# Seven products in place of plain tiles for one more pair in the last pass of a down projection

## The chip, the cores and the metric

The kernel runs on one core of a Trainium2 chip. The metric is the device time of one execution in microseconds (us). A TensorE matmul (PE) takes a stationary tile of 128x128 and a moving tile of 128x512; VectorE is called DVE, ScalarE ACT, GpSimd POOL, and SP is the engine that issues most of the loads.

## The reference

One layer on 256 rows of width 2048: a mixing block (differential attention and a convolution), and then a gated feed-forward block. Only the end of the second one is touched by the change:

```python
h = h + mixed @ w_out
hn = rms_norm(h, norm2_g)
a, bu = hn @ w_gate, hn @ w_up            # 2048 -> 5632
h = h + (silu(a) * bu) @ w_down           # 5632 -> 2048
```

Everything is float32.

## The kernel before

**Precision.** PE multiplies a rounded float32 type. So each operand is split into a rounded part (hi) and the rest (lo), and a product of two tiles is three matmuls: hi by hi, lo by hi, hi by lo. ACT makes the hi part of a weight tile with a cast; its lo part comes from DVE (the raw tile minus hi) or, where a letter in the order below is a capital, from ACT (the negative of hi's input) and a DMA of POOL that adds the raw weights once more (line 346).

**The feed-forward block.** The 5632 hidden columns are taken in 11 blocks of 512 (numbers 0 to 10), in three groups of 4, 4 and 3 blocks. After each group's gate and up blocks a pass of w_down multiplies what the group has made. In a pass the output's 2048 columns are taken in two halves of 1024, called here half A and half B. A hidden block gives two *pairs* of k-tiles, written (8, 0) and (8, 1) for block 8. The third pass has six: (8, 0), (8, 1), (9, 0), (9, 1), (10, 0), (10, 1).

**Two ways to multiply a pair.** In one half a pair is a 2x2 block product: two row blocks of 128, two k-tiles, two column blocks of 512.

- As a *plain pair* it is two units, "g" and "u" (the two column blocks), of four products each: 12 matmuls a unit, 24 in all. Letters G and U are the same with the lo part of the weights by DMA. One unit's weights are a 512 KB load (`raw`); ACT casts `whi` (L342), DVE makes `wlo` (L351).
- As a *seven-product pair*, unit "s" (a 2x2 scheme of Strassen's kind), it is 7 products, 21 matmuls on L1094 to L1096. Its weights are one 1 MB load (`wb`), and then DVE adds up four sums `wt` (L1061, L1062, L1063), ACT casts `wh` (L1068 and L1072), and DVE makes `wl` (L1076 and L1077). `wb`, `wh` and `wl` have two buffers each, `wt` one. The other operand needs sums as well: the function `pair_forms` copies the transposed activations to `af`, casts them, makes the sums `fs` (L975 to L978), lo parts (L979, L980), a cast of `fs` (ACT, L982) and the lo part of it (L984). A plain pair's activations take a copy and a cast (L955, L957) and one subtraction (L959).

**From a gate and up block to w_down.** When the last matmul of block 10 is done, DVE finishes its gated product (L1215 and L1217, two of each). PE transposes it (L922, four small matmuls for each pair), and `transposed` makes the operands, pair (10, 0) first, then (10, 1).

**What sets the order.** Each engine works through one queue in the order in which the program was written. That order is made by `run_chunks`: before it writes the matmuls of unit t it writes the preparation of units ahead of it (the lo parts of up to three units ahead, the sums `wt` of up to five). Work that comes from activations, such as `transposed`, is a generator; one step of it is written at fixed places inside the matmuls (four in an "s" unit, two in a plain one), and `lag(n)` lets n such places go by. A unit whose activations are not yet written makes the generators go on until they are:

```python
while not c["ready"](c):
    resume()
```

The order of the units is a string for each half. `so_far`, a read of the output so far, shares the buffer of `wt` and is used at the very end.

Of the kernel before, what the change touches and what calls it, by code (L numbers as in the profile page):

```python
# [89 lines left out]

DOWN = (dict(pairs=((1, 0), (1, 1), (2, 0)), order=("sgGsgGgsuUuUu",) * 2),
        dict(pairs=((4, 0), (4, 1), (5, 0)), order=("sgGsgGgsuUuUu",) * 2),
        dict(pairs=((8, 0), (8, 1), (9, 0)), order=("sGsGgsUUu", "sGsGGsUUu")))

RAW_AHEAD = 5
LOAD_AHEAD, DMA_AHEAD, SUMS_AHEAD, HI_AHEAD, LO_AHEAD = 9, 5, 5, 4, 3
# [1244 lines left out]
```

## Time and profile before

| | us |
|---|---|
| median of 3 runs | 1040.02 (1039.77 to 1040.20) |
| profiled execution, its own time | 1041.07 |
| its span on the core | 1039.2 |
| mean granted clock of TensorE | 0.998 |
| PE busy | 1030.1 (99%) |
| DVE busy | 862.3 (83%) |
| ACT busy | 685.6 (66%) |
| POOL busy | 155.4 (15%) |

Matmuls overlap in the profile: each is shown for some 390 ns, though the next one starts sooner. A busy PE of 99% says that it hardly ever waits; the time that one matmul costs is the distance between two starts.

### The profile page before, as it was taken

Reading aid. Unit: us, or ns where it says so; the run is one execution under the profiler, and the core shown is the slowest. Engines: PE = TensorE matmul, PEld = TensorE weight load, DVE = VectorE, ACT = ScalarE, POOL = GpSimd, SP = SyncE. Lnnn points to the kernel's source line nnn. Section 1 sums busy time; section 2 is a strip of 40 time slices with the busy share of each in tenths; the row PEclk is TensorE's granted clock in tenths of the full one; section 3 lists DMA queues with packets and bytes.
Section 4 is the critical chain, followed back from the end, with each engine's and each line's share of the span. In section 5 each row is a group of like instructions: output and inputs, shape, how many; then the busy total and the mean of one; then the engine's idle time right before and its main releaser. Section 6 shows DMA issues by size and latency. Waiting matters only on the chain.

```text
span 1039.2 us, 13042 instructions
## 1 busy us (share of the span) xinstructions
PE 1030.1 (99%) x4641; PEld 850.3 (82%) x4641; DVE 862.3 (83%) x1086; ACT 685.6 (66%) x864; POOL 155.4 (15%) x198
## 2 busy tenths in 40 slices
PE   8999999999999999999999999999999999999998
PEld 6888888888888888788888888888888888888886
DVE  5599989898546699999978789999896697998983
ACT  5855568766856567777556567776765666767761
POOL 0040133411100101001002120010001121101021
PEclk9999999999999999999999999999999999999999
DMA  9867766676566669898889998987969999879896
GB/s 357 302 202 211 238 206 213 187 211 176 163 201 231 230 215 281 241 323 240 257 246 298 257 306 267 309 229 249 307 187 285 300 271 331 235 243 298 250 249 129
DMA packets 65777, 258.05 MB, mean 248 GB/s; under 512 B 7344, under 2 KB 8624, under 8 KB 58288
## 3 DMA queue, kind: packets, MB, share of 16 engines
q1 hardware_dynamic: 48656, 201.34, 53.5%
q0 software_dynamic: 16768, 55.58, 28.2%
q8 instruction: 36, 0.59, 0.2%
q10 hardware_dynamic: 288, 0.29, 0.1%
q14 instruction: 29, 0.24, 0.1%
HBM read 248.80 MB, written 8.39 MB: 247 GB/s over the span
## 4 chain that ended last, share of the span: by engine, by line
PE 95%; DVE 2%; ACT 1%; issue 1%; DMA 1%; POOL 0%; SPq 0%; DVEq 0%
PE q L1116 11%; PE q L1120 11%; PE q L1115 11%; PE acc L387 11%; PE acc L382 11%; PE acc L381 11%; PE q L1094 9%; PE q L1096 8%; PE q L1095 8%; PE ps_a L922 1%; DMA raw<-in_wts_dram 1%; PE ps_s L731 1%; PE ps_o L809 0%; DVE y L596 0%; PE ps_h L859 0%
## 5 line engine op out<-in xcount | busy, mean ns | idle before, releaser
L342 ACT CAST whi<-raw 128x1024 fp32r<-128x1024 f32 (+1 forms) x261 | 270.3, 1046 | 105.1 <-PE acc L382 42.0
L351 DVE TENSOR_TENSOR wlo<-raw,whi 128x1024 fp32r<-128x1024 f32 (+1 forms) x173 | 209.0, 1218 | 72.9 <-ACT whi L342 71.4
L381 PE MATMUL acc<-whi,lhi 128*128 128x512 f32 x416 | 164.7, 396 | 1.5 <-ACT lhi L243 1.4
L382 PE MATMUL acc<-whi,llo 128*128 128x512 f32 x416 | 162.8, 391 | 0.7 <-DVE llo L244 0.7
L1077 DVE TENSOR_TENSOR wl<-wt,wh 128x2048 fp32r<-128x2048 f32 x58 | 132.7, 2287 | 20.6 <-ACT wh L1072 20.6
L1068 ACT CAST wh<-wb 128x1536 fp32r<-128x1536 f32 x58 | 86.0, 1483 | 87.5 <-PE q L1095 49.1
L346 POOL DMA_DIRECT2D wlo<-in_wts_dram x74 | 65.0, 889 | 510.4 <-ACT wlo L345 483.6
L1115 PE MATMUL q<-whi,chi 128*128 128x512 f32 x320 | 124.7, 390 | 0.0
L1116 PE MATMUL q<-whi,clo 128*128 128x512 f32 x320 | 124.6, 389 | 0.0
L1072 ACT CAST wh<-wt 128x2048 fp32r<-128x2048 f32 x58 | 110.4, 1904 | 18.5 <-DVE wt L1063 18.4
L1094 PE MATMUL q<-wh,fhi 128*128 128x512 f32 x280 | 109.2, 390 | 0.4 <-DVE sum L1199 0.4
L1096 PE MATMUL q<-wl,fhi 128*128 128x512 f32 x280 | 109.0, 389 | 0.0
L1095 PE MATMUL q<-wh,flo 128*128 128x512 f32 x280 | 109.0, 389 | 0.0
L596 DVE SCALAR_TENSOR_TENSOR y<-upad,cw,y 128x256 f32<-128x256 f32 x240 | 100.8, 488 | 5.3 <-ACT y L589 5.3
L1076 DVE TENSOR_TENSOR wl<-wb,wh 128x1536 fp32r<-128x1536 f32 x58 | 101.6, 1752 | 2.3 <-ACT wh L1068 2.3
L387 PE MATMUL acc<-wlo,lhi 128*128 128x512 f32 x368 | 101.4, 397 | 0.2 <-DVE wlo L351 0.2
L381 PEld LDWEIGHTS acc<-whi,lhi 128*128 128x128 f32 x416 | 78.5, 189 | 18.5 <-ACT lhi L243 1.8
L382 PEld LDWEIGHTS acc<-whi,llo 128*128 128x128 f32 x416 | 78.5, 189 | 17.3 <-DVE llo L244 1.2
L1120 PE MATMUL q<-wlo,chi 128*128 128x512 f32 x320 | 86.9, 393 | 0.0
L387 PEld LDWEIGHTS acc<-wlo,lhi 128*128 128x128 f32 x368 | 68.9, 189 | 14.6 <-DVE wlo L351 0.6
L345 ACT ACTIVATE wlo<-raw 128x1024 fp32r<-128x1024 f32 x74 | 78.1, 1056 | 0.0
L1061 DVE TENSOR_TENSOR wt<-wb 128x1024 f32<-128x1024 f32 x58 | 70.8, 1221 | 1.8 <-DMA wb<-in_wts_dram 1.3
(224 smaller groups left out, 1732.5 us busy)
## 6 DMA issues: line engine op xcount, KB each, us to landing
raw<-in_wts_dram SPq DMA_DIRECT2D x259, 512.0 KB, 5.6
wb<-in_wts_dram SPq DMA_DIRECT2D x57, 1024.0 KB, 8.1
wlo<-in_wts_dram POOLq DMA_DIRECT2D x74, 512.0 KB, 9.3
lod<-in_wts_dram POOLq DMA_DIRECT2D x14, 512.0 KB, 5.8
out_dram<-sum POOLq DMA_DIRECT2D x22, 256.0 KB, 7.2
h<-in_x_dram SPq DMA_DIRECT2D x4, 512.0 KB, 8.4
out_dram<-h POOLq DMA_DIRECT2D x8, 256.0 KB, 4.7
xt<-in_xt_dram SPq DMA_DIRECT2D x7, 256.0 KB, 6.9
```

The source lines that it names most:

```text
L342: act.copy(c["hi"], c["raw"])
L351: dve.tensor_tensor(c["lo"], c["raw"], c["hi"].bitcast(F32), ALU.subtract)
L381: pe.matmul(ps[m], xhi[:, ms], hi[:, j, :], start=c["first"] and j == 0, stop=False)
L382: pe.matmul(ps[m], xlo[:, ms], hi[:, j, :], start=False, stop=False)
L387: pe.matmul(ps[m], xhi[:, ms], lo[:, j, :], start=False, stop=c["last"] and j == nk - 1)
L1077: dve.tensor_tensor(c["lo"][:, :4], c["t"], c["hi"][:, :4].bitcast(F32), ALU.subtract)
L1094: pe.matmul(ps, fhi[:, f, p, :], c["hi"][:, w], start=bool(first), stop=False)
L1095: pe.matmul(ps, flo[:, f, p, :], c["hi"][:, w], start=False, stop=False)
L1096: pe.matmul(ps, fhi[:, f, p, :], c["lo"][:, w], start=False, stop=bool(last))
L1115: pe.matmul(ps, plain[i][0][:, ms], hi[:, i, :], start=i == 0 and bool(c["first"].get(qs[m])), stop=False)
L1116: pe.matmul(ps, plain[i][1][:, ms], hi[:, i, :], start=False, stop=False)
L1120: pe.matmul(sum_bank(c, qs[m]), plain[i][0][:, ms], lo[:, i, :], start=False, stop=i == 1 and bool(c["last"].get(qs[m])))
```

## The change

One line of the table of passes, with the pairs that get seven products and the order of the units of half A and half B:

```diff
-        dict(pairs=((8, 0), (8, 1), (9, 0)), order=("sGsGgsUUu", "sGsGGsUUu")))
+        dict(pairs=((8, 0), (8, 1), (9, 0), (10, 0)), order=("sGsgssUu",) * 2))
```

So pair (10, 0), which comes from the last gate and up block, becomes a seven-product pair. Each half has eight units in place of nine:

| half A | units in order |
|---|---|
| before | s(8,0) G(9,1) s(8,1) G(10,0) g(10,1) s(9,0) U(9,1) U(10,0) u(10,1) |
| now | s(8,0) G(9,1) s(8,1) g(10,1) s(9,0) s(10,0) U(9,1) u(10,1) |

A half has 4 x 21 + 4 x 12 = 132 matmuls where it had 3 x 21 + 6 x 12 = 135. Units with the lo part by DMA are 4 in both halves together, where they were 9; the weights are the same 12 MB, in eight 512 KB and eight 1 MB loads in place of twelve and six.

The order of the queues moves with it. **DVE, from the last weights of s(8,1) on.** Before (`sum` is block 10's gated product, the first `llo` at the end is that of (10, 0)):

```order
L1215 TENSOR_TENSOR sum_8250<-q_7987,sum_8250 128x512
L1215 TENSOR_TENSOR sum_8252<-q_8167,sum_8252 128x512
L1217 TENSOR_TENSOR sum_8250<-sum_8250,sum_8212 128x512
L1217 TENSOR_TENSOR sum_8252<-sum_8252,sum_8251 128x512
L1061 TENSOR_TENSOR wt<-wb 128x1024
L1062 TENSOR_TENSOR wt<-wb,wt 128x512
L1063 TENSOR_TENSOR wt<-wt,wb 128x512
L351 TENSOR_TENSOR wlo<-raw,whi 128x1024
L1076 TENSOR_TENSOR wl<-wb,wh 128x1536
L1077 TENSOR_TENSOR wl<-wt,wh 128x2048
L959 TENSOR_TENSOR llo<-ac,lhi 128x512
```

Now, from the same place of DVE's queue:

```order
L1061 TENSOR_TENSOR wt<-wb 128x1024
L1062 TENSOR_TENSOR wt<-wb,wt 128x512
L1063 TENSOR_TENSOR wt<-wt,wb 128x512
L1215 TENSOR_TENSOR sum_8239<-q_7987,sum_8239 128x512
L1215 TENSOR_TENSOR sum_8241<-q_8165,sum_8241 128x512
L1217 TENSOR_TENSOR sum_8239<-sum_8239,sum_8208 128x512
L1217 TENSOR_TENSOR sum_8241<-sum_8241,sum_8240 128x512
L351 TENSOR_TENSOR wlo<-raw,whi 128x1024
L1076 TENSOR_TENSOR wl<-wb,wh 128x1536
```

The sums `wt` for s(9,0) stood behind the gated product and stand ahead of it now.

**DVE, on to the activations of (10, 1).** Now, further down the same queue, from the end of the weights of s(10,0); `fs` and `llo` are the forms of (10, 0), the three `wt` rows are the sums for s(8,0) of half B, and `alo` is the lo part of (10, 1):

```order
L1077 TENSOR_TENSOR wl<-wt,wh 128x2048
L975 SCALAR_TENSOR_TENSOR fs<-af 128x128
L976 SCALAR_TENSOR_TENSOR fs<-fs,af 128x128
L977 TENSOR_TENSOR fs<-af 128x128
L978 TENSOR_TENSOR fs<-af,fs 128x128
L979 TENSOR_TENSOR llo<-af,lhi 128x2x128
L980 SCALAR_TENSOR_TENSOR llo<-af,lhi 128x128
L1061 TENSOR_TENSOR wt<-wb 128x1024
L1062 TENSOR_TENSOR wt<-wb,wt 128x512
L1063 TENSOR_TENSOR wt<-wt,wb 128x512
L984 TENSOR_TENSOR llo<-fs,lhi 128x4x128
L959 TENSOR_TENSOR alo<-ac,ahi 128x512
```

Where the first `llo` stood right behind the weights of s(9,0), the lo part of (10, 1) now stands behind the sums and weights of s(10,0), the forms of (10, 0) and the sums for half B.

**ACT, over the same stretch.** Before, from the second half of the cast for s(9,0):

```order
L1072 CAST wh<-wt 128x2048
L955 COPY ac<-ps_a 128x512
L957 CAST lhi<-ac 128x512
L342 CAST whi<-raw 128x1024
L345 ACTIVATE wlo<-raw 128x1024
L955 COPY ac<-ps_a 128x512
L957 CAST lhi<-ac 128x512
```

Now, from the casts for s(10,0):

```order
L1068 CAST wh<-wb 128x1536
L1072 CAST wh<-wt 128x2048
L969 COPY af<-ps_a 128x512
L971 CAST lhi<-af 128x2x128
L972 ACTIVATE lhi<-af 128x128
L982 CAST lhi<-fs 128x4x128
L342 CAST whi<-raw 128x1024
L955 COPY ac<-ps_a 128x512
L957 CAST ahi<-ac 128x512
```

The copy and cast of (10, 1) (L955, L957) now stand behind the casts for s(10,0) and all casts of the forms of (10, 0); `ac` has the buffer of `fs`, so L955 also waits until DVE's L984 has read it.

On PE the four transposes of (10, 1) stand right ahead of the unit g(10,1), whose second matmul is the first to need `alo`; before, those of (10, 1) stood right ahead of G(10,0).

## The prediction

> **What bounds the kernel now.** I read the page first (engine totals), then the list of PE's waits, and then the timelines of PE, DVE and ACT over the third pass. From the page, and from PE's waits:
>
> ```profile
> span 1039.2 us, 13042 instructions
> PE 1030.1 (99%) x4641; PEld 850.3 (82%) x4641; DVE 862.3 (83%) x1086; ACT 685.6 (66%) x864; POOL 155.4 (15%) x198
> PE q L1116 <- DVE llo L959: 0.6, 2, 0.4
> ```
>
> PE is the bound: it is busy all through, and in the third pass it waits twice, both times for a lo part of block 10. The price of a matmul is the distance of two starts; PE's last units:
>
> ```profile
> 1026.56 0.39 PE L1115 MATMUL q<-whi,lhi 128*128 128x512 f32 x1
> ...
> 1034.27 0.61 PE L1120 MATMUL q<-wlo,lhi 128*128 128x512 f32 x2
> 1034.92 0.76 DVE L1249 TENSOR_TENSOR sum<-q,sum 128x256 f32<-128x256 f32 x2 [0.60 <-PE q L1120]
> ```
>
> From the first of these starts to the other are 34 matmuls, 7.71 / 34 = 0.227 us each. But DVE is close behind in this pass (us of the stretch, then busy time of PE, PEld, DVE, ACT, POOL):
>
> ```profile
> 971.00:1002.00 31.00, 30.43 (x137) 24.47 (x136) 27.54 (x27) 23.72 (x25) 2.59 (x3) 1.00 0.93 274
> ```
>
> In half A of the pass DVE works 27.5 of 31.0 us. What the change puts on DVE there decides, and in which order. The places it meets, on PE (half A before: s(8,0) ends at 976.2, then G(9,1), s(8,1) from 979.39, G(10,0) from 984.52):
>
> ```profile
> 975.71 0.40 PE L1095 MATMUL q<-wh,llo 128*128 128x512 f32 x1
> 978.02 0.60 PE L922 MATMUL ps_a<-ident,sum 128*128 128x128 f32 x4
> 979.39 0.40 PE L1094 MATMUL q<-wh,lhi 128*128 128x512 f32 x1
> 983.71 0.39 PE L1095 MATMUL q<-wh,llo 128*128 128x512 f32 x1
> 984.52 0.48 PE L1115 MATMUL q<-whi,lhi 128*128 128x512 f32 x1
> 985.37 0.50 PE L1116 MATMUL q<-whi,llo 128*128 128x512 f32 x1 [0.38 <-DVE llo L959]
> 987.99 0.39 PE L1115 MATMUL q<-whi,lhi 128*128 128x512 f32 x1
> 988.57 0.50 PE L1116 MATMUL q<-whi,llo 128*128 128x512 f32 x1 [0.19 <-DVE llo L959]
> ```
>
> and on DVE:
>
> ```profile
> 974.64 1.28 DVE L1215 TENSOR_TENSOR sum<-q,sum 128x512 f32<-128x512 f32 x2
> 975.84 1.29 DVE L1217 TENSOR_TENSOR sum<-sum,sum 128x512 f32<-128x512 f32 x2
> 977.04 1.22 DVE L1061 TENSOR_TENSOR wt<-wb 128x1024 f32<-128x1024 f32 x1
> 979.63 1.22 DVE L351 TENSOR_TENSOR wlo<-raw,whi 128x1024 fp32r<-128x1024 f32 x1
> 980.76 1.75 DVE L1076 TENSOR_TENSOR wl<-wb,wh 128x1536 fp32r<-128x1536 f32 x1
> 982.43 2.29 DVE L1077 TENSOR_TENSOR wl<-wt,wh 128x2048 fp32r<-128x2048 f32 x1
> 984.63 0.69 DVE L959 TENSOR_TENSOR llo<-ac,lhi 128x512 fp32r<-128x512 f32 x1
> ```
>
> DVE has no gap from 974.64 on. From start to start a pair's sums `wt` (L1061 to L1063) take 2.59, its `wl` 1.67 + 2.20 = 3.87, one `wlo` 1.13, the two L1215 and two L1217 1.20 each. So a seven-product pair costs DVE 6.46 us and PE 21 x 0.227 = 4.77; a plain pair costs DVE at most 2.26.
>
> **The change part by part.** *Matmuls taken away.* Two halves, three each: 6 x 0.227 = 1.36 us. Also gone with G(10,0) is the second of the two waits: 987.99 to 988.57 is 0.58, 0.35 more than a matmul.
>
> *The gated product later.* DVE's queue now has the 2.59 of sums for s(9,0) ahead of L1215 and L1217. Up to 974.64 the order is as before. So the last L1217 is written at 974.64 + 2.59 + 2.40 + 0.09 = 979.72, where it was 977.13. PE's transposes L922, which ran at 978.02 without a wait, start at 979.77: PE waits 1.75, and s(8,1) with all behind it starts at 981.14.
>
> *The weights of s(10,0), ahead of the forms.* DVE goes on from 979.63 with the `wlo` of g(10,1) and the `wl` of s(9,0), 5.00 together: 984.63. The sums for s(10,0) end at 987.22. Its `wh` has to take the buffer of s(8,1), so ACT's cast waits for PE. The rows of ACT, and those of DVE for the forms of (9, 0) as the price of those of (10, 0):
>
> ```profile
> 976.19 1.48 ACT L1068 CAST wh<-wb 128x1536 fp32r<-128x1536 f32 x1 [3.13 <-issue]
> 979.75 1.91 ACT L1072 CAST wh<-wt 128x2048 fp32r<-128x2048 f32 x1 [0.17 <-DVE wt L1063]
> 981.56 0.58 ACT L955 COPY ac<-ps_a 128x512 f32<-128x512 f32 x1
> 982.17 0.62 ACT L957 CAST lhi<-ac 128x512 fp32r<-128x512 f32 x1
> ```
>
> ```profile
> 939.29 0.28 DVE L975 SCALAR_TENSOR_TENSOR fs<-af 128x128 f32<-128x128 f32 x1
> ...
> 940.76 1.75 DVE L1076 TENSOR_TENSOR wl<-wb,wh 128x1536 fp32r<-128x1536 f32 x1
> ...
> 944.63 0.69 DVE L984 TENSOR_TENSOR llo<-fs,lhi 128x512 fp32r<-128x512 f32 x1
> ```
>
> L1068 began 0.48 after the start of the last L1095 that read the buffer (975.71 to 976.19). The last L1095 of s(8,1) is now at 983.71 + 1.75 = 985.46, so L1068 runs from 985.94 to 987.42, L1072 to about 989.3; DVE's L1076 starts at 987.5, L1077 runs from 989.35 to 991.55.
>
> *The lo part of (10, 1), which PE needs first.* Behind that stand, in DVE's queue, the six instructions of the forms (939.29 to 940.76: 1.47, to 993.0), the sums for half B (2.59, to 995.6) and L984 (0.69, to 996.3). Only then may ACT's L955 write its buffer; L955 and L957 take 0.61 + 0.62 (to 997.6), L959 starts, and 0.74 after its start (984.63 to 985.37) PE may go on: 998.35. Without the queue PE would be at that matmul at 984.52 + 0.23 + 1.75 = 986.5. It waits some 12 us, and all other units of the pass are behind it, for PE works in order; nothing else has matmuls. Against before this matmul is 998.35 - 985.37 = 12.98 later. The `wb` for half B's sums has to be there at 993.0. Each `wb` is issued when a `wl` has read the old buffer: that of s(9,0) at 961.11, this one at 982.54.
>
> ```profile
> 961.11 0.33 SPq L1055 DMA_DIRECT2D wb<-in_wts_dram  x1
> 982.54 0.33 SPq L1055 DMA_DIRECT2D wb<-in_wts_dram  x1
> DMA to landing us min/median/max: 5.1/7.9/13.8
> ```
>
> The median gives 990.4, in time; the longest 996.3, 3.3 us late (that of s(9,0) lands by 969.0, at the longest 974.9, for its sums at 974.64). I take 0 and keep 3.3.
>
> *The clock after the wait.* No wait of 12 us lies in this trace. The nearest row is the start of the kernel, where PE waited 1.36 and 0.74 us within 8 to 11.2 us:
>
> ```profile
> 12.44 0.59 PE L381 MATMUL acc<-whi,lhi 128*128 128x512 f32 x1
> ...
> 15.82 0.44 PE L381 MATMUL acc<-whi,lhi 128*128 128x512 f32 x1
> 12.00:16.00 4.00, 4.00 (x12) 3.13 (x11) 3.48 (x6) 2.34 (x5) 0.00 (x0) 0.57 1.01 373
> ```
>
> The granted clock was 0.57 from 12 to 16, and 8 matmuls took 3.38 us, 1.57 more than 8 x 0.227. I take 1.57 once, behind the long wait; 0 and 3.1 (twice) are the ends, the second because the wait of 1.75 lies near those gaps in size too. The Trainium skill ("TensorE: Matmul & The Clock Gate", part 1, what's actually happening) says that a free-running window of about 3.4 us has to be busy before the full clock comes back; then 3.4 to 6.8 us run at half clock and cost 1.7 to 3.4, and the sum below would be 0.1 to 1.8 us more.
>
> *Half B.* I set its clock at the moment when PE ends s(9,0) of half A, which frees `wh`. Then DVE has: `wl` of s(8,0) done at 5.5 (behind ACT's 1.48 and 1.91), sums 8.1, the bank sums of half A 3.98 (before: L1196 at 999.25, the next L1076 at 1003.23), `wl` of s(8,1) at 15.9, sums 18.5, two L1249 like the L1215 19.7, one `wlo` 20.9, `wl` of s(9,0) 24.7, sums 27.3, ACT's L1072 1.91, L1077 2.20: 31.5.
>
> ```profile
> 999.25 0.68 DVE L1196 TENSOR_TENSOR sum<-q,sum 128x512 f32<-128x512 f32 x1
> 1003.23 1.75 DVE L1076 TENSOR_TENSOR wl<-wb,wh 128x1536 fp32r<-128x1536 f32 x1
> ```
>
> PE has 132 matmuls to the start of s(10,0) of half B, 29.9 us, and its third needs that `wl` at 30.4: it waits 1.1. The other units find theirs ready (the closest is s(9,0), 24.7 against 25.6). Ends: 0, and 3.3 if a load is late here.
>
> *The end.* `so_far` needs the buffer of `wt`, so it is issued when that last L1077 is done, at 31.5 on half B's clock.
>
> ```profile
> so_far<-out_dram POOLq DMA_DIRECT2D x1, 512.0 KB, 7.1
> ```
>
> It lands at 38.6, two instructions of 0.6 that add it run to 39.8, and PE's last matmuls, 42 behind the third of s(10,0), end past 41: 0, at most 1. The five DMAs of lo parts less, and five ACT copies, free engines that nobody waits for: 0.
>
> *Sum.* 12.98 - 1.36 - 0.35 + 1.57 + 1.1 = 13.9 us. The profiled span would be 1053.1, and its own time was 1041.07, 1.05 above the median of the runs; on the median 1040.02 + 13.9 = 1053.9.
>
> **Rivals.** *Not slower:* the lo part of (10, 1) comes in time because DVE runs ahead. Then 1.36 is won, or with the two waits (984.52 to 985.37 is 0.62 more than a matmul) 1.36 + 0.35 + 0.62: 1037.7 to 1038.7. It takes L959 done by 984.75, 13.6 us ahead of the sum; two pairs' weights (6.46 each) would have to be off DVE's queue, and the order has them there. *The link through `wh` and `ac` is loose* (casts early, clock not reduced, half B without a wait): DVE's queue alone is 979.63 + 5.00 + 6.46 + 1.47 + 2.59 + 0.69 = 995.8, with ACT and L959 997.8; 12.4 - 1.71 gives 1050.7. *A load is late* at one of the two places, or the clock stays down longer: 1053.9 + 3.3 = 1057.2, with both more.
>
> **Chances.** About the sum, 1051.5 to 1056: 0.65; the loose link, 1049.5 to 1051.5: 0.14; late loads or clock, 1056 to 1060: 0.15; not slower: 0.03; between, where the wait is only half: 0.03. The range from 1049.5 to 1058 leaves out less than 2 in 10. A change under 0.2% (2.1 us) is about what cannot be told from none; 1.36 alone is 0.13%, so half of "not slower" is "the same".
>
> **What would show it.** Right: in the profile after, PE waits once for DVE's L959 on `alo` for 10 to 13 us near 986, once about 1.7 us for L1217, the clock drops in the slices behind it, and s(10,0) of half B waits about 1 us for L1077. Wrong: L959 starts before 990, or PE's wait names a load.

## The result, and the profile after

| | before | changed |
|---|---|---|
| median of 5 runs, us | 1040.03 (1039.77 to 1040.20) | 1064.02 (1061.06 to 1064.37) |
| profiled execution: own time, span | 1041.07, 1039.2 | 1061.06, 1059.3 |
| first to last matmul of the third pass, profiled | 971.31 to 1034.27: 62.96 | 970.33 to 1054.49: 84.16 |

The changed kernel is slower: the ratio is 1.0223, with a 95% interval from 1.0211 to 1.0235. The direction was as forecast. The size was not: 24.0 us where 13.9 were forecast, and the time lies 6 us above the upper end of the range.

The profile after, first its span and engines from the page, and then the list of PE's waits from 970 us on (us in total, times, longest):

```profile
span 1059.3 us, 13015 instructions
PE 1033.2 (98%) x4635; PEld 851.6 (80%) x4635; DVE 878.6 (83%) x1103; ACT 684.3 (65%) x861; POOL 149.8 (14%) x193
```

```profile
PE q L1115 <- ACT ahi L957: 6.7, 1, 6.7
PE q L1094 <- DVE sum L1249: 5.1, 1, 5.1
PE ps_a L922 <- ACT af L969: 3.7, 1, 3.7
PE q L1094 <- DVE sum L1215: 2.5, 1, 2.5
```

Before, PE waited 0.6 us in this pass; now 18.0. Where these waits stand, in PE's timeline (start, duration; the bracket is the idle time before the row and what ended it):

```profile
974.18 0.39 PE L1096 MATMUL q<-wl,lhi 128*128 128x512 f32 x1
977.11 0.50 PE L1094 MATMUL q<-wh,lhi 128*128 128x512 f32 x1 [2.54 <-DVE sum L1215]
...
985.65 0.39 PE L1096 MATMUL q<-wl,lhi 128*128 128x512 f32 x1
989.70 1.11 PE L922 MATMUL ps_a<-ident,sum 128*128 128x128 f32 x4 [3.66 <-ACT af L969]
997.52 0.79 PE L1115 MATMUL q<-whi,ahi 128*128 128x512 f32 x1 [6.71 <-ACT ahi L957]
998.25 0.80 PE L1116 MATMUL q<-whi,alo 128*128 128x512 f32 x1
998.84 0.63 PE L1115 MATMUL q<-whi,ahi 128*128 128x512 f32 x1
...
1003.11 0.48 PE L1094 MATMUL q<-wh,lhi 128*128 128x512 f32 x1
...
1022.03 0.39 PE L1096 MATMUL q<-wl,lhi 128*128 128x512 f32 x1
1027.50 0.79 PE L1094 MATMUL q<-wh,lhi 128*128 128x512 f32 x1 [5.08 <-DVE sum L1249]
...
1030.64 0.40 PE L1115 MATMUL q<-whi,lhi 128*128 128x512 f32 x1
```

From distances of starts less 0.227 a matmul (0.09 a transpose), the pass loses: 2.7 ahead of 977.11; 3.8 + 7.5 ahead of the unit g(10,1) at 997.52; 2.9 in that unit, whose 12 matmuls take 997.52 to 1003.11, 5.59 us where 2.72 are full speed (0.5 of it ahead of the second matmul, which needs `alo`, and 2.4 at half clock behind it, mostly 0.43 from start to start); 5.2 ahead of 1027.50; and 1.5 in the seven matmuls behind it. That is 23.6. Before's pass was 1.25 longer than its units are without a wait (62.96 against 61.71, e6 below), and 1.36 of matmuls are gone: 23.6 - 1.25 - 1.36 = 21.0, against 84.16 - 62.96 = 21.2.

The stretch of half A whose row stands in the prediction, now (busy time of PE, PEld, DVE, ACT, POOL, then the granted clock):

```profile
971.00:1002.00 31.00, 18.09 (x70) 13.71 (x69) 25.80 (x29) 14.72 (x16) 1.73 (x2) 0.80 0.60 190
```

PE works 18.1 of 31.0 us, where it had 30.4, and DVE hardly less than before. DVE in detail:

```profile
975.76 0.69 DVE L1063 TENSOR_TENSOR wt<-wt,wb 128x512 f32<-128x512 f32 x1
976.37 1.28 DVE L1215 TENSOR_TENSOR sum<-q,sum 128x512 f32<-128x512 f32 x2
...
989.20 2.29 DVE L1077 TENSOR_TENSOR wl<-wt,wh 128x2048 fp32r<-128x2048 f32 x1
...
997.50 0.69 DVE L959 TENSOR_TENSOR alo<-ac,ahi 128x512 fp32r<-128x512 f32 x1 [1.36 <-ACT ahi L957]
...
1009.46 1.76 DVE L1076 TENSOR_TENSOR wl<-wb,wh 128x1536 fp32r<-128x1536 f32 x1 [10.13 <-ACT wh L1068]
...
1020.18 1.75 DVE L1076 TENSOR_TENSOR wl<-wb,wh 128x1536 fp32r<-128x1536 f32 x1
...
1026.76 1.28 DVE L1249 TENSOR_TENSOR sum<-q,sum 128x512 f32<-128x512 f32 x2
```

Two things are new here. DVE, the engine everything waits for up to 998, then stands idle for 10.13 us: its next work is the `wl` of half B's first unit, whose `wh` waits for a buffer that PE's units still hold, and PE is late. And the two L1249, which read half A's last PSUM banks, stand behind the `wl` of s(8,1) and the sums for s(9,0) of half B (1020.18 to 1026.76). PE's seventh product of s(8,0), Q3, goes into one of these banks.

### The profile page after: what moved, and what is told of

Read it like the earlier page. It is cut to its first block, busy times and chain, and to the rows that moved or that the text cites. A ratio compares the mean times of both kernels' runs of the same rounds, so it can differ in the third digit from the quotient of the medians.

```text
span 1059.3 us, 13015 instructions
## 1 busy us (share of the span) xinstructions
PE 1033.2 (98%) x4635; PEld 851.6 (80%) x4635; DVE 878.6 (83%) x1103; ACT 684.3 (65%) x861; POOL 149.8 (14%) x193
## 4 chain that ended last, share of the span: by engine, by line
PE 89%; DVE 5%; DMA 2%; ACT 2%; issue 1%; POOL 0%; SPq 0%; DVEq 0%; ACTq 0%
PE q L1115 11%; PE q L1116 11%; PE q L1120 11%; PE acc L387 10%; PE acc L382 10%; PE acc L381 10%; PE q L1094 8%; PE q L1095 8%; PE q L1096 8%; DMA raw<-in_wts_dram 1%; DVE wl L1077 1%; PE ps_a L922 1%; DMA xt<-in_xt_dram 1%; DVE wt L1061 1%; ACT wh L1072 1%
## 5 line engine op out<-in xcount | busy, mean ns | idle before, releaser
L342 ACT CAST whi<-raw 128x1024 fp32r<-128x1024 f32 (+1 forms) x257 | 266.0, 1045 | 99.5 <-PE acc L382 46.1
L1068 ACT CAST wh<-wb 128x1536 fp32r<-128x1536 f32 x60 | 89.0, 1483 | 109.1 <-PE q L1095 61.0
L1077 DVE TENSOR_TENSOR wl<-wt,wh 128x2048 fp32r<-128x2048 f32 x60 | 137.2, 2287 | 16.3 <-ACT wh L1072 16.0
L346 POOL DMA_DIRECT2D wlo<-in_wts_dram x69 | 60.1, 871 | 518.9 <-ACT wlo L345 495.6
L1072 ACT CAST wh<-wt 128x2048 fp32r<-128x2048 f32 x60 | 114.3, 1905 | 20.5 <-DVE wt L1063 20.4
L1076 DVE TENSOR_TENSOR wl<-wb,wh 128x1536 fp32r<-128x1536 f32 x60 | 105.1, 1752 | 16.1 <-ACT wh L1068 16.1
L1094 PE MATMUL q<-wh,fhi 128*128 128x512 f32 x280 | 109.1, 390 | 0.4 <-DVE sum L1199 0.4
L382 PEld LDWEIGHTS acc<-whi,llo 128*128 128x128 f32 x416 | 78.4, 189 | 18.2 <-DVE llo L244 2.2
L387 PEld LDWEIGHTS acc<-wlo,lhi 128*128 128x128 f32 x368 | 68.4, 188 | 14.3 <-DVE wlo L351 0.6
L1061 DVE TENSOR_TENSOR wt<-wb 128x1024 f32<-128x1024 f32 x60 | 73.2, 1221 | 3.4 <-DMA wb<-in_wts_dram 2.8
L345 ACT ACTIVATE wlo<-raw 128x1024 fp32r<-128x1024 f32 x69 | 72.9, 1056 | 0.0
```

The lines of the kernel that those rows point to most:

```text
L342: act.copy(c["hi"], c["raw"])
L382: pe.matmul(ps[m], xlo[:, ms], hi[:, j, :], start=False, stop=False)
L387: pe.matmul(ps[m], xhi[:, ms], lo[:, j, :], start=False, stop=c["last"] and j == nk - 1)
L1077: dve.tensor_tensor(c["lo"][:, :4], c["t"], c["hi"][:, :4].bitcast(F32), ALU.subtract)
L1094: pe.matmul(ps, fhi[:, f, p, :], c["hi"][:, w], start=bool(first), stop=False)
```

## The experiments

Each kernel's ratio is to runs of the kernel before on the same chip (1040.17 to 1040.22 median). "Below the changed kernel" compares medians from different chips, on which the kernel before differs by 0.2 us at most. The changed kernel's median lies 3.0 us above its profiled run, so not all of such a difference is in the traces. What they show is the length of the third pass: 84.16 us in the changed kernel, 80.10 in e1, 80.15 in e2, 85.17 in e3, 74.00 in e4, 63.12 in e5, 72.33 in e7 and 84.30 in e8.

**Half A's last sums first** (e1_bank_first; at half A's last unit the preparation of later units waits, so that on DVE the two L1249 stand ahead of `wl` and sums; nothing else moves):

```
-until("part", part_of, t + 1 + LO_AHEAD)
+until("part", part_of, t + 1 + (0 if chunks[t].get("hold") else LO_AHEAD))
-until("sums", sums_of, t + 1 + (SUMS_AHEAD if t >= first else 0), ...
+until("sums", sums_of, t + 1 + (SUMS_AHEAD if t >= first and not chunks[t].get("hold") else 0), ...
-... down_done(n, sums, last), prompt=True)
+... down_done(n, sums, last), prompt=True, hold=g == 2)
```

> Only DVE's queue is changed: at the last unit of half A the preparation of later units is held back, so the two L1249, which read half A's last bank, stand ahead of the weights of s(8,1) and the sums of s(9,0) of half B; same instructions, and PE, ACT, POOL and SP keep their order. Theory A (the second wait of PE is DVE's queue order around the bank of the last product): PE's wait of 5.2 us for L1249 at 1022 to 1027.5 goes, with the 1.6 us of half clock behind it; a wait of about 1.5 us for L1077 comes back ahead of s(10,0) of half B; 5 to 6 us faster than the changed kernel, 1056 to 1058. Theory B (DVE simply has too much work in this pass, the order only says where PE waits): the same 5 us show up as waits for later weights, 1061 to 1064.

Measured: 1058.10 (1057.51 to 1059.62), ratio 1.0173 [1.0158, 1.0188], 5.9 below the changed kernel. Its DVE timeline and the new ones of PE's waits:

```profile
1021.18 1.28 DVE L1249 TENSOR_TENSOR sum<-q,sum 128x512 f32<-128x512 f32 x2
```

```profile
PE q L1096 <- DVE wl L1077: 1.4, 1, 1.4
PE q L1096 <- DVE wl L1076: 0.5, 1, 0.5
```

L1249 starts 5.6 us earlier and PE no longer waits for it; 0.5 and 1.4 us come back at the two lo parts of s(10,0), its third and its sixth matmul. So the wait for L1249 is the order in DVE's queue, not an amount of work.

**(10, 1) in place of (10, 0) as the fourth pair** (e2_pair_10_1):

```
-pairs=((8, 0), (8, 1), (9, 0), (10, 0))
+pairs=((8, 0), (8, 1), (9, 0), (10, 1))
```

> The fourth seven-product pair is (10,1) in place of (10,0), so the plain unit g is (10,0), whose lo part stands right behind the weights of the fourth pair in DVE's queue, ahead of the forms and of half B's sums. Theory A (the first wait ends when DVE's queue reaches that lo part): L959 at about 991.4, PE's second matmul of g at 992.1 in place of 998.25, so 6 us less waiting, and 1056 to 1058; the wait for L1249 in half B stays at 5 us. Theory B (too much DVE work): the forms come later instead and PE waits the same time ahead of s(10,1), 1061 to 1064.

Measured: 1057.75 (1057.16 to 1059.49), ratio 1.0170 [1.0155, 1.0186], 6.3 below the changed kernel. PE's timeline and waits:

```profile
992.44 0.79 PE L1116 MATMUL q<-whi,alo 128*128 128x512 f32 x1 [0.90 <-DVE alo L959]
```

```profile
PE q L1094 <- ACT lhi L982: 3.0, 1, 3.0
PE q L1094 <- DVE sum L1249: 2.5, 1, 2.5
```

The plain unit behind s(8,1) gets its lo part at 992.4 instead of 998.2, since the forms no longer stand ahead of it in the queues. The forms are late now, but the unit that needs them comes later (L982: 3.0). The wait for L1249 was expected to stay at 5 us and is 2.5.

**PE kept at work in the long wait** (e3_fill; the four transposes of (10, 1) are made ten times over):

```
-transpose_two(pt, aa, t)
+[transpose_two(pt, aa, t) for _ in range(10 if (j, t) == (10, 1) else 1)]
```

> PE makes the four transposes of (10,1) ten times over (the same values into the same bank) in the time in which it waits for L957 and L959. Theory A (the half clock behind the wait is the price of the idle time itself): the 12 matmuls of g(10,1), which took 5.6 us, take 2.7; L959 stays at 997.5; 2 to 3 us faster than the changed kernel, and less spread between runs, 1058 to 1061. Rival (the clock has another cause, or the long wait costs nothing beyond itself): no change, 1061 to 1064.

Measured: 1062.17 (1060.36 to 1062.76), ratio 1.0207 [1.0192, 1.0222]. In PE's timeline:

```profile
977.20 0.73 PE L1094 MATMUL q<-wh,lhi 128*128 128x512 f32 x1 [2.53 <-DVE sum L1215]
977.73 0.63 PE L1095 MATMUL q<-wh,llo 128*128 128x512 f32 x1
...
991.38 6.02 PE L922 MATMUL ps_a<-ident,sum 128*128 128x128 f32 x40 [3.66 <-ACT af L969]
999.20 0.49 PE L1115 MATMUL q<-whi,ahi 128*128 128x512 f32 x1 [1.80 <-ACT ahi L957]
...
1003.74 0.63 PE L1094 MATMUL q<-wh,lhi 128*128 128x512 f32 x1
```

The unit took 4.5 us instead of 5.6, with full speed from 1000.27 to 1001.19, so filling the wait may have kept part of the clock. But the time lies in the rival's range, not in Theory A's, and this run does not compare cleanly: its clock fell already behind the first wait (977.20 to 977.73 is 0.53 for a matmul; behind the changed kernel's wait of the same length it stayed up), so that s(8,1) ended 1.6 us later and the chain through `wh` with it. The granted clock is the eighth value of these stretches, first of the changed kernel, then of this one:

```profile
975.00:980.00 5.00, 2.89 (x14) 2.39 (x15) 4.93 (x8) 2.08 (x2) 0.00 (x0) 1.00 0.65 267
```

```profile
975.00:980.00 5.00, 2.80 (x7) 2.25 (x8) 4.93 (x9) 1.56 (x2) 0.00 (x0) 0.73 0.66 270
```

So this run does not show what filling the wait is worth. It gave the next question: is the first wait what spreads the changed kernel's runs over 3.3 us (below, e8)?

**The plain unit later in half A** (e4_g_later):

```
-order=("sGsgssUu",) * 2
+order=("sGssgsUu", "sGsgssUu")
```

> Half A in the order s(8,0) G(9,1) s(8,1) s(9,0) g(10,1) s(10,0) U u, so PE has 21 more matmuls ahead of the unit that waits. Theory A (a fixed moment in DVE's and ACT's queues ends the wait): L959 still starts at 997 to 998.5, PE's wait of 11.3 us shrinks by the 4.8 us of s(9,0); 1057 to 1060. Theory B (DVE work in all): 1061 to 1064, the time comes back as waits for the weights of s(10,0) or of half B.

Measured: 1051.47 (1050.84 to 1053.34), ratio 1.0113 [1.0096, 1.0130], 12.5 below the changed kernel, twice what was expected. The part that was not expected is in DVE's timeline and PE's waits:

```profile
998.91 1.76 DVE L1076 TENSOR_TENSOR wl<-wb,wh 128x1536 fp32r<-128x1536 f32 x1 [0.68 <-ACT wh L1068]
```

```profile
PE q L1094 <- DVE sum L1249: 1.4, 1, 1.4
```

With s(9,0) ahead of the plain unit, PE gives its `wh` back while it waits for nothing, and DVE makes half B's first `wl` at 998.91, not at 1009.46. Half B's wait shrinks from 5.1 to 1.4 though half B itself was not edited. So a late operand is paid twice: by PE, which waits, and by DVE, whose next work needs the buffers that the waiting PE holds.

The rival that was still standing: whatever the order, DVE and ACT have too much to do in this pass with a fourth pair. Four kernels on that.

**Four pairs with mended queues** (e5_queues; `CUTS` counts back from the last unit: -17 is the last of block 10, -16 the first of half A, -9 its last; each gives how many units less far ahead lo parts, sums and casts are written):

```
-pairs=((8, 0), (8, 1), (9, 0), (10, 0)), order=("sGsgssUu",) * 2
+pairs=((8, 0), (8, 1), (9, 0), (10, 1)), order=("sGsGssUU", "sGsGsusU")
+CUTS = {-17: (2, 0, 0, 0), -16: (0, 4, 3, 0), -9: (3, 0, 0, 0)}
-until("part", part_of, t + 1 + LO_AHEAD)
+until("part", part_of, t + 1 + max(0, LO_AHEAD - CUTS.get(t - n, (0, 0, 0, 0))[0]))
...
-yield from lag(TO_TRANSPOSE)
+yield from lag(2 if j == 10 else TO_TRANSPOSE)
(in transposed, for block 10: lag(3) to lag(2), lag(2) to lag(0))
```

> Four seven-product pairs as in the changed kernel, but the fourth is (10,1), the halves are s(8,0) G(9,1) s(8,1) G(10,0) s(9,0) s(10,1) U U and s G s G s u s U, block 10's transposes and their copies are written earlier, and the preparation is written fewer units ahead at three places (end of block 10, first and last unit of half A). The amount of arithmetic is that of the changed kernel. Theory A (the loss is waits made by the order in the queues): the waits for L1215 (2.5 us), L969 (no loss seen), L957 (6.7 + 3.7 ahead of it) and L1249 (5.2) go, and with them the 4.5 us at half clock; some 1 us each of waits for L984 and for sums of half A stay: 1064 - 23.5 + 2 to 3 = 1041 to 1044. Theory B (DVE and ACT have too much to do in this pass with a fourth pair: some 6.2 us more of sums and lo parts for each half, less 2.3 for the unit pair it replaces, that is 8 us for both halves and 2 of forms): the waits only move to other operands, at least 8 us of them stay: above 1049.

Measured: 1043.31 (1042.90 to 1044.03), ratio 1.0030 [1.0019, 1.0042]: 20.7 of the 24.0 us are gone with the same products. (DVE's work is not quite the same: seven units, where the changed kernel has four, have their lo part from ACT and a DMA.) All of PE's waits in the pass, its last matmuls, and the engines' busy times from 965 to 1060 us, here and then in the changed kernel:

```profile
PE q L1095 <- DVE llo L984: 0.5, 1, 0.5
PE q L1094 <- DVE sum L1199: 0.4, 1, 0.4
PE q L1096 <- DVE wl L1077: 0.2, 1, 0.2
```

```profile
1034.26 0.61 PE L1120 MATMUL q<-wlo,ahi 128*128 128x512 f32 x2
```

```profile
sum 95.00, PE 68.59 PEld 54.75 DVE 66.26 ACT 40.58 POOL 11.34; mean PE 5.72 PEld 4.56 DVE 5.52 ACT 3.38 POOL 0.95
```

```profile
sum 95.00, PE 72.11 PEld 57.57 DVE 69.23 ACT 37.75 POOL 8.73; mean PE 6.01 PEld 4.80 DVE 5.77 ACT 3.15 POOL 0.73
```

The granted clock is 1.00 from 965 to 1030. PE's pass takes 971.14 to 1034.26, 63.12 us, as long as before's 62.96: the 1.36 of matmuls taken away are paid back in small waits, because DVE, which had gaps before (it was busy for 2.0 of the 5 us from 990 on), now has hardly any up to 1010.

**Three pairs with mended queues** (e6_before_queues; the kernel before, with the same `CUTS` at the same three places and the same lags, orders of the units unchanged; with nine units in a half the places are -19, -18 and -10):

> The kernel before with three seven-product pairs, and only the order edits of the last one: block 10's transposes earlier, fewer units ahead at the same three places; orders of the units unchanged. If order alone gives what the four-pair version gains over the changed kernel, this one, with 6 matmuls (1.36 us) more and fewer sums, loses the kernel before's waits in the pass (1.4 + 0.7 us ahead of the first units after the activations, part of them hidden by nothing) and perhaps 0.7 us of half clock: 1038.5 to 1039.5, 0.1% below before. Rival: before's waits in the pass were unavoidable: 1040.2, the same as before within 0.05%. If an earlier transposition only makes PE wait for L1217: 1041 to 1043.

Measured: 1039.43 (1038.48 to 1040.04), ratio 0.9990 [0.9981, 0.9999]. PE waits nowhere in the pass, which takes 970.48 to 1032.19, 61.71 us:

```profile
1032.19 0.61 PE L1120 MATMUL q<-wlo,lhi 128*128 128x512 f32 x2
```

```profile
sum 95.00, PE 67.81 PEld 55.80 DVE 53.52 ACT 39.16 POOL 13.18; mean PE 5.65 PEld 4.65 DVE 4.46 ACT 3.26 POOL 1.10
```

This is the fastest of all kernels here, by a hair that its interval just clears. With equal care for the queues the fourth pair makes the kernel 3.9 us slower (1043.31 against 1039.43), and DVE has 12.7 us more to do (66.26 against 53.52). Between the two profiled spans (1041.0 and 1037.2) it is 3.8 us: 1.4 in the pass, 0.7 ahead of it (971.14 and 970.48), and 1.7 behind the last matmuls, of which e9 says more. So the rival holds too, but the traces show it for the 1.4 only.

**The change's own pair, with mended queues** (e7_queues_10_0; e5 with (10, 0) for (10, 1) in `pairs`):

> The same order edits as the four-pair version with early transposes, but with the change's own pair (10,0) as the fourth. Theory: the forms of (10,0) (a copy, two casts on ACT and eight instructions on DVE) then stand in the queues ahead of the copy, cast and subtraction of the plain pair (10,1), which the fourth unit needs 10 us into the pass while the forms are needed only 20 us in. So the wait of PE for L957 comes back, 7 to 11 us, and with it about 2.5 us at half clock: 1050 to 1055. Rival: with the look-ahead mended the pick of the pair does not matter: the same as with (10,1) within 1 us.

Measured: 1052.65 (1051.25 to 1053.39), ratio 1.0118 [1.0104, 1.0131], 9.3 above e5. The one wait of PE in the pass:

```profile
PE q L1115 <- ACT ahi L957: 10.0, 1, 10.0
```

So which half of block 10 gets the forms is worth 9 us by itself, through what stands ahead of L959 and L957 in the queues.

**Without the first wait** (e8_first_wait; the changed kernel with `CUTS = {-17: (2, 0, 0, 0)}` alone):

> The changed kernel with one edit: at the last unit of block 10 the lo parts are written one unit ahead in place of three, so that on DVE the two L1215 stand ahead of the lo parts of s(8,0)'s followers, and PE's first wait (2.5 us, L1094 for L1215) goes. What follows is in order and should wait so much longer, 2 to 3 us for L969 and L957 later. Theory A (a 2.5 us wait costs by itself only if the clock drops behind it, as it did in one profiled run of the version with ten transposes): the time is 1060.5 to 1062 and the runs lie within 1 us of one another, where the changed kernel's spread over 3.3 us. Rival (the wait is a plain loss on the critical chain): 1061.5, spread unchanged at 3 us. If the chain behind it is unchanged and the clock is not the cause of the spread: 1064.

Measured: 1061.63 (1061.28 to 1061.89, five runs), ratio 1.0205 [1.0191, 1.0219]. PE's waits:

```profile
PE q L1115 <- ACT ahi L957: 6.7, 1, 6.7
PE ps_a L922 <- ACT af L969: 6.4, 1, 6.4
PE q L1094 <- DVE sum L1249: 5.1, 1, 5.1
```

The 2.5 us went into the next wait (3.7 to 6.4): the sum is 18.2, where it was 18.0. And yet the median fell by 2.4 us and the spread from 3.3 to 0.6. The wait itself had cost nothing in the profiled run of the changed kernel, its fastest; what is gone is what it did in the other runs. That the clock falls behind it, as in e3's profile, fits. So does the mean granted clock on record for each run: 0.991 in the changed kernel's fastest, 0.987 or 0.988 in its four others, 0.989 or 0.990 in all five here. But no trace shows one of the slower runs of the changed kernel, so where their clock fell stays open.

**The last seven-product unit earlier** (e9_last_s; e5 with half B as s G s G s s U u). In e5 PE ends its matmuls when before did, and yet the span is 1.8 us longer:

```
-"sGsGsusU"
+"sGsGssUu"
```

> The four-pair version with mended queues, but half B runs s G s G s s U u, so that two plain units stand behind its last seven-product unit, not one. In that version PE's last matmul started at 1034.26 us of the span, within 0.02 us of the kernel before, and yet the span was 1.8 us longer: the last write of half B's column 1 (256 KB each, two, issued 1032.64) was still on its way when the last four writes were issued, and these took 4.1 us to land in place of 1.9. Theory: with that unit 2.7 us earlier the time from the last matmul to the end falls from 6.7 to 4.9 us or so; the last seven-product unit now waits some 1 to 1.7 us for its L1077: 1042 to 1043, a gain of 0.3 to 1. Rival: the tail is set by something else and the new wait simply adds: 1044 to 1045.

Measured: 1044.14 (1042.64 to 1045.36), ratio 1.0037 [1.0023, 1.0051]. The last four writes (KB each, median us from issue to landing), first in e5, then here, and PE's timeline here:

```profile
out_dram<-sum SPq DMA_DIRECT2D x4, 128.0 KB, 4.1
```

```profile
out_dram<-sum SPq DMA_DIRECT2D x4, 128.0 KB, 1.9
```

```profile
1024.78 0.50 PE L1096 MATMUL q<-wl,lhi 128*128 128x512 f32 x1 [0.97 <-DVE wl L1076]
1027.11 0.80 PE L1096 MATMUL q<-wl,lhi 128*128 128x512 f32 x1 [1.37 <-DVE wl L1077]
1027.71 0.63 PE L1094 MATMUL q<-wh,lhi 128*128 128x512 f32 x1
...
1037.26 0.61 PE L1120 MATMUL q<-wlo,ahi 128*128 128x512 f32 x2
```

The tail did shrink as expected (from the start of the last matmuls to the end of the span 6.7 in e5, 4.8 here), but not in the expected way. The two earlier writes were issued no earlier (1032.66, in e5 1032.64); the last four were issued 2.6 us later (1037.05, in e5 1034.48). That fits final writes that met earlier ones in e5, but no run moves the writes alone. And PE ended 3.0 us later, though it had entered the pass 0.8 earlier, since the unit came too early for DVE and the two waits brought half clock behind them (1027.11 to 1027.71 for one matmul). The forecast of 1042 to 1043 missed; the median lies in the rival's range.

## Why the prediction was right or wrong

**The long wait: right, though its fit to the row is partly luck.** DVE's L1077 for s(10,0) was to start at 989.35 and started at 989.20; L959 was to start at 997.6 and started at 997.50; PE's first matmul with `alo` was put at 998.35 and stands at 998.25. This execution entered the pass 0.98 us earlier than before's, so counted from there the last one is 0.9 later, not 0.1 earlier: the earlier entry and a first wait that was longer than forecast (next point) cancel. The list shows this wait as two, for ACT's L969 and L957, and not for L959, because PE's transposes and the hi part come first on the same chain. e2 and e7 changed what stands ahead of these operands in the queues, and the end of the wait moved, to 992.44 and 993.26; e4 put more matmuls ahead of it on PE, and it stayed, at 997.56.

**The gated product later: right cause, wrong place.** Forecast were 1.75 us at the transposes L922, for L1217; it was 2.54 at L1094, for L1215. DVE's sums for s(9,0) do stand ahead. But L1215 reads a PSUM bank, and the last product of s(8,0) goes into it, ahead of the transposes. In before's trace the bank was already tight, in PE's weight loads:

```profile
975.38 0.19 PEld L1094 LDWEIGHTS q<-wh,lhi 128*128 128x128 f32 x1 [0.25 <-DVE sum L1215]
```

**Half B: the step that failed.** It was put at 1.1 us, s(10,0)'s third matmul for L1077. That wait did not come; 5.2 us were lost at s(8,0), for L1249, and 1.5 at half clock behind it. The prediction's own list of DVE had the two L1249 ending at 19.7 on half B's clock, the first some 0.6 sooner. PE's Q3 product of s(8,0) stands 21 + 12 + 12 + 18 = 63 matmuls, 14.3 us, behind the clock's zero: a wait of about 5 could be read from the same numbers. The list was asked only when each `wl` is ready, and never who waits for the instructions that read PSUM. e1 took this wait away alone and won 5.9 on the medians, 4.1 in the profiled pass. Only then did s(10,0) wait, as forecast but for L1076 too (0.5 and 1.4). Its third matmul reads L1076's part; the first to read L1077's is the sixth, three matmuls later than the prediction had it.

**The clock: mis-sized.** 1.57 once was taken; the profiled run lost 2.4 behind the long wait and 1.5 behind half B's, 3.9 in all. The end "twice", 3.1, was named and not taken, and the second place was half B's wait, which was not foreseen. The Trainium skill ("TensorE: Matmul & The Clock Gate", part 1, what's actually happening) speaks of a window of some 3.4 us; by the prediction's estimate from it, 1.7 to 3.4, the long wait would have been sized right; half B's 1.5 lies just under it.

**The rest.** No load was late: none of PE's waits names one. The end cost nothing: 4.8 us from the start of the last matmuls, before 4.9. The 1.36 of the matmuls is there: with no waits three pairs take 61.71, and e5's 63.12 less its excess of 2.8 over 0.227 a matmul is 60.3. In the profile, half B (+4.1) and the clock (+2.3), less 0.1 at the long wait and 0.1 at the end, make the 6.2 us by which the span passed the forecast 1053.1. The median lies 3.0 above the profiled run; e8, without the first wait, takes 2.4 off the median. No term of the prediction stands for that.

**The rivals.** "Not slower" had the right condition, L959 early, but e5 shows that it is not enough: with all long waits gone PE's pass is as long as before and the end is 1.8 later. "A load is late" did not happen. That the order and not the amount of work makes most of the loss is shown: e4 took 12.5 of the 24.0 us off with the same instructions in another order, and e5 took 20.7 off, with some 3 us less for DVE (66.26 against 69.23). The pick of the pair alone is 9.3 of that (e7).

## What to carry to other kernels

When a change puts work ahead in the queue of an engine with little slack, list for every instruction behind it who waits for it; instructions that read PSUM count like those that make operands, since the next sum into the bank waits for them. A late operand costs a second time where the waiting engine holds buffers that the late engine needs for its next work. A unit that saves matmuls is worth its saving only while the engine that prepares it keeps gaps: here 1.36 us of PE were bought with about 13 us of DVE (e5 against e6), and even with no long wait left it did not pay.

## What was not expected of the hardware

A wait of 2.53 us was followed by half speed in one execution (e3, 0.53 and then 0.43 us a matmul from 977.20 on) and one of 2.54 at the same place by full speed in another (the changed kernel, 977.11). In e9 a wait of 1.37, 2.3 us behind one of 0.97, was followed by half speed from 1027.11 to 1030.22. Behind the same wait of 5.1 us for L1249 half speed cost 1.5 in the changed kernel and 2.7 in e8 (1027.12 to 1033.20 for 15 matmuls). The same page of the Trainium skill, part 1, calls the cold stretch variable from run to run, because the window runs freely, and that agrees; it lets the clock drop after an idle window of about 3.4 us, and here it dropped behind idle times shorter than that.
